# A two-layer attention block: shift rows on SyncE's queue and turned once more per unit, lead maxima in written order, modulation jobs one at a time

## The chip, the cores and the metric

The kernel runs on one core of a Trainium2 chip. The metric is the device time of one execution in microseconds (us). Engines are named as the profile names them: PE (TensorE, matrix products), DVE (VectorE), ACT (ScalarE), POOL (GpSimd) and SP (SyncE, which here only issues DMAs). Each engine runs its own instructions in program order and waits on semaphores for the others.

## The reference, cut to what matters

Two layers over 1024 latent tokens and 256 context tokens, width 1024. Layer 0 is grouped-query attention with 16 heads of 64 and 4 key heads, layer 1 is latent attention with 16 heads. Each has a normalisation that is scaled and shifted by a condition, and a gate path.

```python
def hybrid_layer(x, ctx, c, c_ctx, w_mod, b_mod, norm_w, mixer, mixer_params, cos, sin, with_ctx_out):
    shift, scale, gate = adaln_params(c, w_mod, b_mod)
    shift_c, scale_c, gate_c = adaln_params(c_ctx, w_mod, b_mod)
    h = rms_norm(x, norm_w) * (1.0 + scale[:, None, :]) + shift[:, None, :]
    hc = rms_norm(ctx, norm_w) * (1.0 + scale_c) + shift_c
    y, yc = mixer(h, hc, mixer_params, cos, sin, with_ctx_out)
    x = x + gate[:, None, :] * y
    if with_ctx_out:
        ctx = ctx + gate_c * yc
    return x, ctx

def gqa_attend(q, k, v):
    s = jnp.einsum('bqhgd,bkhd->bhgqk', q, k).astype(jnp.float32) * (GQA_HEAD_DIM ** -0.5)
    p = jax.nn.softmax(s, axis=-1).astype(v.dtype)
    return jnp.einsum('bhgqk,bkhd->bqhgd', p, v)
```

The modulation of layer 1 (`adaln_params`: silu(c) times a matrix) does not depend on layer 0, so the kernel computes it between the work of layer 0.

## The kernel before

**Stages.** A plan (0 to about 262 us) works out norms, projections, query and key rotations and most gates of layer 0: every piece of work is put down with a slot, and the pieces are issued in order of their slots. A tile of queries takes four slots (24 products of PE, then on DVE `hss`, `h_ms`, `t`, `tl` and the scaled `t` of L1123, which PE transposes at L1131), and some tiles carry a piece of a weight split (`wb`, L152). Among them stand the modulation jobs: `cols_fetch` loads a block of layer 1's modulation matrix, `cols_mult` (L1342) multiplies it with the condition of the latent and of the context tokens, by `mod_cols` (L251 to L254): one DVE product over 1024 columns for each, with the sum as a column. Later jobs (`some_cols`) follow until 311 us with the last gate slices.

**Lead.** Then come twelve gate slices (`gate_slice`, 512 or 256 tokens by 128 gate columns, 24 products each, named `mm`), among which the maxima of the first two attention units are to be taken, two after each slice but the last, up to 14 (L1505 to L1519). A maximum (`mx`, L475 for latent keys, L480 for context keys) is a pair of products of queries and keys, and a DVE reduction. PE's order in this stage is the scheduler's.

**Attention of layer 0** (`Attention.run`) goes through 20 units, numbered from 0: 16 heads over all 1280 keys, and four units of context tokens over 256 keys (numbers 4, 9, 18 and 19). For each unit: scores `st` for a block of 128 keys at a time (L589), exponentials `p` on ACT (L596), then the products with v, `avt` (L650). Ahead of the unit that is worked on, the maxima of the units behind it are taken among the scores. The sums of the exponentials are added up on POOL (`acp`, L636), turned on DVE to a row `rrow`, which goes to DRAM and comes back over all rows as `rb`; the gate comes as `sg`; POOL multiplies `rb` with `sg` and the result `os` with `rb` (L733, L734), and `od` (L738) stores it. In PE, DVE, ACT and POOL the order is the written one here; that of SP's DMAs is the scheduler's.

**Shift rows.** Scores are shifted by the maximum before the exponential, by one more product: `st<-shift,minus` (L589), where `shift` holds the negated maxima of four heads as rows. `do_shift` (L499 to L512) reduces a unit's maxima on DVE to `top` and puts a `turn` in a list: four 32 x 32 transposes on DVE (`turn_squares`, L95) and two DMAs (L510) that write the row into `shift`. In layer 0 `shift` is a single tile that all units share: a row's write waits until the products of the unit before have read the tile, and the next unit's first product with it waits for the row. In layer 1 each unit has such rows in a tile `QS` of its own. `run_turns(next_turn)` runs the turns of the list up to unit `next_turn`: the next unit, or the one behind the context units that follow. Before the change it is called once in a unit, between its scores and its products with v. The DMAs go out on ACT's queue while `run` works (`self.running`), else on SP's:

```python
for n in range(2):
    (act if self.running else sp).dma_start(raw(s["crow"][n]), r[4 * n:4 * n + 4, :])
```

**Loads.** Keys of a key head are KA and KB (L1418), queries of a unit QA and QL (L1395, L1396), all on SP's queue. The keys' room in SBUF becomes free when the last modulation job of `some_cols` is done.

Of the kernel before, what the change touches and what calls it, by code (L numbers as in the profile page):

```python
# [12 lines left out]
BF16 = mybir.dt.bfloat16  # L13
# [6 lines left out]
P = 128  # L20
D = 1024
# [8 lines left out]
WIDE = (True, False)  # L30


def raw(ap):
    return ap.bitcast(F32)
# [3 lines left out]
def hybrid_kernel(ctx: ExitStack, tc: tile.TileContext, ins: dict, out: bass.AP):  # L38
    nc = tc.nc
    pe, act, dve, pool, sp = nc.tensor, nc.scalar, nc.vector, nc.gpsimd, nc.sync  # L40
# [50 lines left out]
    def turn_squares(dst, src):  # L91

        w = src.shape[-1]
        for g in range(4):
            dve.transpose(dst[:, w * g:w * g + w], src[32 * g:32 * g + 32, :])  # L95
# [96 lines left out]
    class ModPart:  # L192
# [6 lines left out]
        def __init__(self, l, sec, part, n, pool_of, bufs, rowp, ps_mod, ps_tp):  # L199
            self.l, self.sec, self.part, self.n = l, sec, part, n  # L200
            self.pool_of, self.bufs, self.rowp, self.ps_mod, self.ps_tp = pool_of, bufs, rowp, ps_mod, ps_tp
            self.st = {}
# [45 lines left out]
                dve.tensor_tensor(s1, tv, bias, op=ALU.add)  # L248
                dve.scalar_tensor_tensor(A[l][:, ks, :], s1, 1.0, nw, op0=ALU.add, op1=ALU.mult)

    def mod_cols(w, u, junk, sec, k, conds=2):  # L251

        for j in range(conds):
            dve.scalar_tensor_tensor(junk, w, 0.5, u[:, j, :], op0=ALU.mult, op1=ALU.mult, accum_out=sums_of[sec][:, k, j:j + 1])  # L254

    def mod_cols_end(sec):

        t = sums_of[sec]
        if sec == 2:
            dve.tensor_add(raw(tops[3][:, :KT]), t[:, :, 0], colsT[:, 1, 16:24])  # L260
            r = turned[96:128, :]
            turn_squares(r, raw(tops[3]))
            sp.dma_start(gated[1][0:1, :].rearrange("o (k p) -> (o k) p", p=P), r[:KT, :])
            return
        bias = colsT[:, 1, 8 * sec:8 * sec + 8].unsqueeze(2).broadcast_to([P, KT, 2])
        if sec == 0:
            dve.tensor_tensor(Bv[1], t, bias, op=ALU.add)
        else:
            nw = colsT[:, 1, 24:32].unsqueeze(2).broadcast_to([P, KT, 2])
            dve.tensor_tensor(t, t, bias, op=ALU.add)  # L270
            dve.scalar_tensor_tensor(A[1], t, 1.0, nw, op0=ALU.add, op1=ALU.mult)
# [77 lines left out]
    class Attention:  # L349
        def __init__(self, l, units, ops):  # L350
            self.l, self.units, self.ops = l, units, ops
            self.state = {}
            self.vcache = {}
            self.kcache = {}
            self.sm = sm_pool
            self.step = 0
            self.deferred = []
            self.totals = []
            self.sums = 0
            self.running = False  # L360
            self.turns = []
            self.started = 0
            self.done = 0
            self.todo = []
            self.last_lat = [u for u in units if u["kind"] == "lat"][-1]
# [133 lines left out]
        def do_shift(self, u):  # L499

            s = self.state[id(u)]
            m = tops[self.units.index(u) % 4]
            dve.reduce_max(m[:, :8], s["m"], axis=AX.X)

            def turn():
                at_ = 32 * (self.units.index(u) % 2)
                r = turned[at_:at_ + 32, :]
                turn_squares(r, raw(m))
                for n in range(2):
                    (act if self.running else sp).dma_start(raw(s["crow"][n]), r[4 * n:4 * n + 4, :])  # L510

            self.turns.append((self.units.index(u), turn))  # L512

# [232 lines left out]
        def run(self, lead, ahead, extra, tail):  # L746

            count = lead
            parts = None
            self.running = True  # L750
            with tc.manual_schedule(engines={mybir.EngineType.PE, mybir.EngineType.DVE, mybir.EngineType.Activation, mybir.EngineType.Pool}):
                for t, u in enumerate(self.units):
                    kts = u["kts"]
# [6 lines left out]
                    next_turn = t + 1  # L760
                    while next_turn + 1 < len(self.units) and len(self.units[next_turn]["kts"]) <= 4:
                        next_turn += 1
                    if not WIDE[self.l]:
                        next_turn = None

                    def one_more():
# [156 lines left out]
    right = dict(side="right", reuse_waits="tile")  # L923
# [7 lines left out]
    small = stR.enter_context(tc.tile_pool(name="sml0", bufs=3, **right))  # L931
# [5 lines left out]
    plan = Plan()  # L937
# [379 lines left out]
    gate_in = {}  # L1317
# [21 lines left out]
        sp.dma_start(w, ins["l1_w_mod_t"][sec * D + k * P:sec * D + (k + 1) * P, :])  # L1339
        gate_in[k] = w  # L1340

    def cols_mult(sec, k):  # L1342
        mod_cols(gate_in.pop(k), gate_in["u"], small.tile([P, D], BF16, name="junk", tag="junk", bufs=1), sec, k)

    plan.at(46, more_room)
    at_step = 47.6
# [10 lines left out]
    for j in range(2):  # L1357
        plan.at(72.5 + 4 * j, cond_rows, j)
    for k in range(KT):
        plan.at(77 + 7 * k, cols_fetch, 0, k)  # L1360
        plan.at(82.2 + 7 * k, cols_mult, 0, k)
    plan.at(138, mod_cols_end, 0)
    weight("g1", 2048, 120, (120.2, 122.2, 124.2, 127.2), (125.2, 127.1, 129.2, 132.2))
    for m in range(2):
# [109 lines left out]
    at = Attention(0, units, dict(scale=0.125, load=l0_load, scores=l0_scores, maxima=l0_maxima, mparts=1, open=l0_open, gaps=(4, 8, 11), kbufs=2, qbufs=3, vw=256))  # L1474
# [3 lines left out]
    u = mw.tile([P, 2, D], F32, name="urow", tag="urow", bufs=1)  # L1478
    for j in range(2):
        sp.dma_start(u[:, j, :], ud[j:j + 1, :].broadcast_to([P, D]))  # L1480
    junk = mw.tile([P, D], BF16, name="junk", tag="junk", bufs=1)
    blocks = [(sec, k) for sec in (1, 2) for k in range(KT)]

    def some_cols(n):

        for _ in range(n):
            sec, k = blocks.pop(0)
            w = mw.tile([P, D], F32, name="wcols", tag="wcols")
            sp.dma_start(w, ins["l1_w_mod_t"][sec * D + k * P:sec * D + (k + 1) * P, :])
            mod_cols(w, u, junk, sec, k, 3 - sec)  # L1490
            if k == KT - 1:
                mod_cols_end(sec)

    with tc.tile_pool(name="wkg0a", bufs=4, **right) as wkg:
        for m in range(2, 4):
            for s0 in range(0, NT, 512):
                gate_slice(0, 0, m, s0, min(512, NT - s0), ws["g0"], hT, ps_mm, wkg)
                some_cols(2)
# [7 lines left out]
        pieces.pop(0)()()  # L1506
    stG.close()
    at.open_early(stE)
    at.start_unit()
    with tc.tile_pool(name="wkg0b", bufs=2, **right) as wkg:  # L1510
        for m in range(4):
            for s0 in range(0, NT, 512) if m else (1024,):
                gate_slice(0, 1, m, s0, min(512, NT - s0), ws["g1"], hT, ps_mm, wkg)
                if (m, s0) != (3, 1024):
                    at.maxima(min(at.done + 2, 14), 2)
                at.step += 1
                at.run_turns()
                if s0 == 512:
                    pieces.pop(0)()()  # L1519
# [5 lines left out]
    first = []  # L1525
# [47 lines left out]
    with ExitStack() as st:  # L1573
# [3 lines left out]
        small = st.enter_context(tc.tile_pool(name="sml1a", bufs=3, **right))  # L1577
# [56 lines left out]
    with ExitStack() as st:  # L1634
# [3 lines left out]
        small = st.enter_context(tc.tile_pool(name="sml1b", bufs=3, **right))  # L1638
# [180 lines left out]
    for p_ in range(8):  # L1819
        for par in range(2):  # L1820
# [3 lines left out]
    at = Attention(1, units, dict(scale=float(96 ** -0.5), load=l1_load, scores=l1_scores, maxima=l1_maxima, mparts=2, open=l1_open, gaps=(4, 6, 9),  # L1824
                                  kbufs=3, qbufs=3, vw=128))
    stE = ExitStack()

    with ExitStack() as st:
# [3 lines left out]
        small = st.enter_context(tc.tile_pool(name="sml1c", bufs=3, **right))  # L1832
# [145 lines left out]
    first = []  # L1978
# [57 lines left out]
```

## Time and profile before

| | us |
|---|---|
| median of three runs (lowest, highest) | 1651.92 (1649.15, 1654.16) |
| the profiled execution | 1649.71 |
| its span on the core | 1647.9 |

| engine | busy us | share of the span |
|---|---|---|
| PE | 1603.8 | 97% |
| DVE | 1142.0 | 69% |
| POOL | 957.7 | 58% |
| ACT | 642.2 | 39% |

PE is nearly always at work. In the page's row of the granted clock every slice reads 9, so the losses are small and scattered: they are read from PE's waits by cause and from windows of 20 us. In a row of the timeline the columns are the start, the duration, the engine, the line, the operation, the tiles (out <- in), and in brackets how long the engine was idle before it and what ended that. "SPq" and "ACTq" are instructions that issue a DMA: their duration is the issue, not the transfer.

### The profile page before, as it was taken

Reading aid. Unit: us, or ns where it says so; the run is one execution under the profiler, and the core shown is the slowest. Engines: PE = TensorE matmul, PEld = TensorE weight load, DVE = VectorE, ACT = ScalarE, POOL = GpSimd, SP = SyncE. Lnnn points to the kernel's source line nnn. Section 1 sums busy time; section 2 is a strip of 40 time slices with the busy share of each in tenths; the row PEclk is TensorE's granted clock in tenths of the full one; section 3 lists DMA queues with packets and bytes.
Section 4 is the critical chain, followed back from the end, with each engine's and each line's share of the span. In section 5 each row is a group of like instructions: output and inputs, shape, how many; then the busy total and the mean of one; then the engine's idle time right before and its main releaser. Section 6 shows DMA issues by size and latency. Waiting matters only on the chain.

```text
span 1647.9 us, 26555 instructions
## 1 busy us (share of the span) xinstructions
PE 1603.8 (97%) x9836; PEld 1181.2 (72%) x9836; DVE 1142.0 (69%) x1939; ACT 642.2 (39%) x943; POOL 957.7 (58%) x628
## 2 busy tenths in 40 slices
PE   8999899999999999989999999999999999999998
PEld 5776788775555555557887899887766767767587
DVE  3765986678898888716566667765788788788231
ACT  4643221125554655422234543341534444435310
POOL 2773540118899899933334555450768778777521
PEclk9999999999999999999999999999999999999999
DMA  9545667851444332257324776777566565563451
GB/s 320 178 137 180 186 186 234 247 144 46 107 96 107 97 98 78 59 145 223 119 77 131 214 234 174 221 204 196 127 150 143 136 136 121 136 144 76 124 182 66
DMA packets 215358, 246.26 MB, mean 149 GB/s; under 512 B 19962, under 2 KB 157426, under 8 KB 215228
## 3 DMA queue, kind: packets, MB, share of 16 engines
q1 hardware_dynamic: 214260, 244.31, 53.3%
q8 instruction: 78, 1.28, 0.3%
q14 instruction: 52, 0.43, 0.1%
q10 hardware_dynamic: 968, 0.25, 0.1%
HBM read 170.71 MB, written 73.63 MB: 148 GB/s over the span
## 4 chain that ended last, share of the span: by engine, by line
PE 81%; DVE 6%; DMA 5%; POOL 4%; issue 2%; ACT 1%; SPq 1%; ACTq 0%; DVEq 0%; POOLq 0%
PE st L589 19%; PE av L650 8%; PE mm L109 7%; PE avt L650 7%; PE mm L110 7%; PE mm L111 7%; PE mx L441 4%; PE y L109 3%; PE y L111 3%; PE y L110 3%; PE mx L475 2%; DVE wb L152 1%; POOL acp L636 1%; PE mx L451 1%; DVE t L1123 1%
## 5 line engine op out<-in xcount | busy, mean ns | idle before, releaser
L636 POOL TENSOR_TENSOR acp<-acp,p 128x1024 f32<-128x1024 f32 x188 | 448.8, 2387 | 12.6
L596 ACT ACTIVATE p<-st 128x1024 f32<-128x1024 f32 x328 | 336.4, 1027 | 165.0 <-PE st L589 156.4
L443 DVE TENSOR_REDUCE m<-mx 128x1 f32<-128x512 f32 x256 | 175.6, 691 | 65.3 <-PE mx L441 59.4
L636 POOL TENSOR_TENSOR acp<-p 128x1024 f32<-128x1024 f32 x34 | 81.5, 2398 | 201.3 <-ACT p L596 201.2
L484 DVE TENSOR_REDUCE m<-mx 128x1 f32<-128x1024 f32 x128 | 150.8, 1220 | 45.6 <-PE mx L475 44.7
L650 PE MATMUL avt<-p,v 128*64 128x512 f32 x672 | 149.4, 596 | 0.0
L650 PE MATMUL av<-p,v 128*64 128x512 f32 x640 | 141.1, 595 | 0.0
L152 POOL TENSOR_TENSOR wb<-wraw,wa 128x512 fp32r<-128x512 f32 (+3 forms) x65 | 91.1, 1415 | 77.3 <-ACT wa L173 77.2
L109 PE MATMUL mm<-wa,hh 128*128 128x512 f32 (+2 forms) x336 | 125.5, 373 | 2.0 <-ACT hh L1023 2.0
L589 PE MATMUL st<-QH,KH 64*128 64x512 f32 x320 | 122.7, 407 | 0.1
L111 PE MATMUL mm<-wa,hl 128*128 128x512 f32 (+2 forms) x336 | 120.9, 360 | 1.4 <-DVE hl L1026 1.4
L110 PE MATMUL mm<-wb,hh 128*128 128x512 f32 (+2 forms) x336 | 120.6, 359 | 0.0
L589 PE MATMUL st<-QH,KL 64*128 64x512 f32 x320 | 118.1, 391 | 0.0
L589 PE MATMUL st<-QL,KH 64*128 64x512 f32 x320 | 117.7, 390 | 0.0
L109 PE MATMUL y<-wa,oh 128*128 128x512 f32 (+1 forms) x296 | 114.1, 386 | 2.0 <-DVE yt L880 1.4
L111 PE MATMUL y<-wa,ol 128*128 128x512 f32 (+1 forms) x296 | 113.5, 384 | 0.6 <-DVE ol L863 0.6
L110 PE MATMUL y<-wb,oh 128*128 128x512 f32 (+1 forms) x296 | 113.5, 383 | 0.0
L650 PEld LDWEIGHTS avt<-p,v 128*64 128x64 f32 x672 | 46.3, 137 | 93.2 <-issue 85.0
L650 PEld LDWEIGHTS av<-p,v 128*64 128x64 f32 x640 | 44.4, 137 | 87.9 <-issue 87.3
L109 PE MATMUL mm<-hh,wa 128*128 128x512 f32 (+1 forms) x264 | 104.0, 394 | 0.0
L110 PE MATMUL mm<-hl,wa 128*128 128x512 f32 (+1 forms) x264 | 102.5, 388 | 0.0
L111 PE MATMUL mm<-hh,wb 128*128 128x512 f32 (+1 forms) x264 | 102.1, 387 | 0.0
(259 smaller groups left out, 4026.7 us busy)
## 6 DMA issues: line engine op xcount, KB each, us to landing
wraw<-in_l_w_in SPq DMA_DIRECT2D x28, 512.0 KB
wcols<-in_l_w_mod_t SPq DMA_DIRECT2D x24, 512.0 KB
KH<-k1h SPq DMA_DIRECT2D x32, 320.0 KB
KL<-k1l SPq DMA_DIRECT2D x32, 320.0 KB
rb<-rrow SPq DMA_DIRECT2D x72, 128.0 KB
mraw<-in_l_w_mod SPq DMA_DIRECT2D x16, 512.0 KB
wraw<-in_l_w_out SPq DMA_DIRECT2D x16, 512.0 KB
QA<-q0h SPq DMA_DIRECT2D x32, 256.0 KB
```

Of the source, the lines that this page charges most:

```text
L109: pe.matmul(ps, lhsT=lh(k), rhs=rh(k), start=first and i == 0, stop=False)
L110: pe.matmul(ps, lhsT=lh(k), rhs=rl(k), start=False, stop=False)
L111: pe.matmul(ps, lhsT=ll(k), rhs=rh(k), start=False, stop=last and i == len(ks) - 1)
L152: eng.tensor_sub(lo, a, b)
L441: pe.matmul(held["m"][:, cs], lhsT=q[:, t * P:(t + 1) * P], rhs=k[:, ks], start=j == 0, stop=j == len(pairs) - 1)
L443: dve.reduce_max(s["m"][:, i, n:n + 1], held["m"], axis=AX.X)
L475: pe.matmul(m[:, n * 512:n * 512 + 512], lhsT=q[:, i * P:(i + 1) * P], rhs=k[:, n * 512:n * 512 + 512], start=True, stop=True)
L484: dve.reduce_max(s["m"][:, i, 0:1], m, axis=AX.X)
L589: pe.matmul(ps[:, n * 512:(n + 1) * 512], lhsT=lh, rhs=rh, start=j == 0, stop=j == last)
L596: act.activation(p, ps, AF.Exp, scale=self.ops["scale"])
L636: pool.tensor_add(t, a, b)
L650: pe.matmul(s["av"][64 * n:64 * n + 64, :], lhsT=s["v"][:, kt, u["vc"]:u["vc"] + 64], rhs=p[:, n * 512:(n + 1) * 512], start=kt == kts[0], ...
```

## The change

Four things are changed.

1. The rows of `turn` go out on SP's queue always, in both layers (`self.running` is gone).
2. In `run`, for layer 0 (`WIDE`), `run_turns(next_turn)` is called at the start of each unit too, ahead of its scores. `next_turn` is the next unit, or the one behind the context units that follow.
3. In the lead, both units are started at once, PE's order is the written one, and the slices (0, 1024) and (1, 0) carry no maxima: the first two stand behind slice (1, 512).
4. The modulation jobs of the plan are one product at a time: five blocks are at 82.2 + 8k and four slots later, the other three at 121.5 + 5(k - 5) and two slots later, where there was a pair at 82.2 + 7k.

```diff
-    def mod_cols(w, u, junk, sec, k, conds=2):
-
-        for j in range(conds):
+    def mod_cols(w, u, junk, sec, k, conds):
+
+        for j in conds:
             dve.scalar_tensor_tensor(junk, w, 0.5, u[:, j, :], op0=ALU.mult, op1=ALU.mult, accum_out=sums_of[sec][:, k, j:j + 1])
...
-                    (act if self.running else sp).dma_start(raw(s["crow"][n]), r[4 * n:4 * n + 4, :])
+                    sp.dma_start(raw(s["crow"][n]), r[4 * n:4 * n + 4, :])
...
-                    if not WIDE[self.l]:
+                    if WIDE[self.l]:
+                        self.run_turns(next_turn)
+                    else:
                         next_turn = None
...
-    def cols_mult(sec, k):
-        mod_cols(gate_in.pop(k), gate_in["u"], small.tile([P, D], BF16, name="junk", tag="junk", bufs=1), sec, k)
+    def cols_mult(sec, k, j):
+        mod_cols(gate_in[k], gate_in["u"], small.tile([P, D], BF16, name="junk", tag="junk", bufs=1), sec, k, (j,))
...
-        plan.at(77 + 7 * k, cols_fetch, 0, k)
-        plan.at(82.2 + 7 * k, cols_mult, 0, k)
+        first = 82.2 + 8 * k if k < 5 else 121.5 + 5 * (k - 5)
+        plan.at(first - 5, cols_fetch, 0, k)
+        for j in range(2):
+            plan.at(first + (4 if k < 5 else 2) * j, cols_mult, 0, k, j)
...
-    at.start_unit()
-    with tc.tile_pool(name="wkg0b", bufs=2, **right) as wkg:
+    for _ in range(2):
+        at.start_unit()
+    with tc.tile_pool(name="wkg0b", bufs=2, **right) as wkg, tc.manual_schedule(engines={mybir.EngineType.PE}):
         for m in range(4):
             for s0 in range(0, NT, 512) if m else (1024,):
                 gate_slice(0, 1, m, s0, min(512, NT - s0), ws["g1"], hT, ps_mm, wkg)
-                if (m, s0) != (3, 1024):
+                if (m, s0) > (1, 0) and (m, s0) != (3, 1024):
                     at.maxima(min(at.done + 2, 14), 2)
```

**SP's queue behind unit 6.** Before the change, SP's rows stand so from the store of unit 3 on (`128x2x256` is the store of unit 4, the context unit; QA and QL are the queries of a unit that is loaded ahead):

```order
L738 DMA od_109<-os 64x512 x2
L728 DMA sg<-sgd_107 64x512 [waits DMAHW4_49,DMAHW1_49,Pool_49]
L738 DMA od_109<-os 128x2x256 [waits Pool_49]
L728 DMA sg<-sgd_107 64x512
L1395 DMA QA<-q0h 64x1024 [waits PE_49]
L1396 DMA QL<-q0l 64x512 [waits DMAHW5_49,PE_49]
L1395 DMA QA<-q0h 64x1024 [waits DMAHW7_49]
L702 DMA rrow<-turned 32x32 [waits DMAHW1_49,DVE_49]
```

and after it:

```order
L737 DMA od_109<-os 64x512 [waits DMAHW7_49]
L737 DMA od_109<-os 64x512 [waits DMAHW0_49]
L727 DMA sg<-sgd_107 64x512 [waits DMAHW4_49,DMAHW1_49,Pool_49]
L737 DMA od_109<-os 128x2x256 [waits Pool_49]
L727 DMA sg<-sgd_107 64x512
L1397 DMA QA<-q0h 64x1024 [waits PE_49]
L509 DMA shift<-turned 1x4x128 [waits DMAHW5_49,DVE_49,PE_49]
L509 DMA shift<-turned 1x4x128 [waits DMAHW6_49,PE_49]
L1398 DMA QL<-q0l 64x512 [waits DMAHW7_49]
L701 DMA rrow<-turned 32x32 [waits DMAHW0_49,DVE_49]
```

The two rows of `shift` (L509 there; the change takes a line out above) were not on SP. Now they stand behind the gate loads `sg`, behind the store `od` that waits for POOL, and behind the first half of a QA load.

**PE in the lead.** Before the change, PE's rows at the first maximum (the products of slice (2, 0), with `hh`, on both sides of it):

```order
L109 MATMUL mm<-hh,wa 128x512
L110 MATMUL mm<-hl,wa 128x512
L111 MATMUL mm<-hh,wb 128x512
L475 MATMUL mx<-KA,QA 128x512 [waits DMAHW7_49,DMAHW3_49,PE_49]
L475 MATMUL mx<-KA,QA 128x512
L109 MATMUL mm<-hh,wa 128x512
L110 MATMUL mm<-hl,wa 128x512
L111 MATMUL mm<-hh,wb 128x512
L109 MATMUL mm<-hh,wa 128x512
```

and after it (the products of slice (1, 512) ahead, and those of (1, 1024), with `hhc`, behind):

```order
L109 MATMUL mm<-hh,wa 128x512
L110 MATMUL mm<-hl,wa 128x512
L111 MATMUL mm<-hh,wb 128x512
L474 MATMUL mx<-KA,QA 128x512 [waits DMAHW7_49,DMAHW3_49,PE_49]
L474 MATMUL mx<-KA,QA 128x512 [waits DMAHW5_49,DMAHW0_49]
L474 MATMUL mx<-KA,QA 128x512 x2
L109 MATMUL mm<-hhc,wa 128x256 [waits DVE_49]
L110 MATMUL mm<-hlc,wa 128x256
L111 MATMUL mm<-hhc,wb 128x256
```

The first maximum stood behind half of slice (2, 0), with one maximum at a place; now two stand together behind slice (1, 512), with slice (1, 1024) and all of (2, 0) behind them.

**DVE among the query tiles.** Before the change, where the first job stands (`junk` is the product of a job):

```order
L103 TENSOR_TENSOR tl<-tp,th 128x512 [waits DMAHW3_49,Activation_49]
L254 SCALAR_TENSOR_TENSOR junk,cols_69<-wcols,urow 128x1024 [waits DMAHW5_49]
L254 SCALAR_TENSOR_TENSOR junk,cols_69<-wcols,urow 128x1024 [waits DVE_49]
L1123 TENSOR_TENSOR t_1829<-t_1829,h_rs 128x512 [waits Pool_49]
L1104 TENSOR_REDUCE hss<-sq 128x8 [waits Activation_49]
L133 TENSOR_SCALAR h_ms<-hss 128x8 [waits DVE_49]
L1110 TENSOR_TENSOR t_1883<-mm,rope_q 128x512 [waits DMAHW2_49]
L1116 TENSOR_TENSOR t_1885<-mm,rope_q 128x16x16 x2
```

and after it:

```order
L103 TENSOR_TENSOR tl<-tp,th 128x512 [waits DMAHW3_49,Activation_49]
L254 SCALAR_TENSOR_TENSOR junk,cols_69<-wcols,urow 128x1024 [waits DMAHW5_49]
L1123 TENSOR_TENSOR t_1829<-t_1829,h_rs 128x512 [waits DVE_49,Pool_49]
L1104 TENSOR_REDUCE hss<-sq 128x8 [waits Activation_49]
L133 TENSOR_SCALAR h_ms<-hss 128x8 [waits DVE_49]
L1110 TENSOR_TENSOR t_1880<-mm,rope_q 128x512 [waits DMAHW2_49]
L1116 TENSOR_TENSOR t_1882<-mm,rope_q 128x16x16 x2
L103 TENSOR_TENSOR tl<-tp,th 128x512 [waits DMAHW7_49,Activation_49]
L254 SCALAR_TENSOR_TENSOR junk,cols_69<-wcols,urow 128x1024
L1123 TENSOR_TENSOR t_1880<-t_1880,h_rs 128x512 [waits Pool_49]
```

The second product of the job moved behind the `tl` of the next tile.

More of the change, by code (lines that the diff above doesn't have):

```diff
@@ L359, in __init__ @@
             self.sums = 0
-            self.running = False
             self.turns = []
@@ L749, in run @@
             parts = None
-            self.running = True
             with tc.manual_schedule(engines={mybir.EngineType.PE, mybir.EngineType.DVE, mybir.EngineType.Activation, mybir.EngineType.Pool}):
@@ L1489, in some_cols @@
             sp.dma_start(w, ins["l1_w_mod_t"][sec * D + k * P:sec * D + (k + 1) * P, :])
-            mod_cols(w, u, junk, sec, k, 3 - sec)
+            mod_cols(w, u, junk, sec, k, range(3 - sec))
             if k == KT - 1:
```

## The prediction

> **What bounds the kernel now.** I read the page first, then PE's waits by cause, then the windows in which those waits lie, then the timelines around each.
>
> ```profile
> span 1647.9 us, 26555 instructions
> ...
> PE 1603.8 (97%) x9836; PEld 1181.2 (72%) x9836; DVE 1142.0 (69%) x1939; ACT 642.2 (39%) x943; POOL 957.7 (58%) x628
> ```
>
> TensorE is busy 97% of the span. The change removes no matmul, so it can gain only what PE loses to waiting and to its clock, and it can lose any amount by a new wait. PE's waits by cause (total us, times, longest):
>
> ```profile
> PE tp L1131 <- DVE t L1123: 7.6, 7, 2.3
> PE st L589 <- DMA shift<-turned: 7.6, 3, 5.1
> ...
> PE mx L475 <- issue: 2.8, 1, 2.8
> ...
> PE mx L475 <- DMA QA<-q0h: 1.1, 1, 1.1
> ```
>
> These four are the ones that the change touches: the query phase of layer 0 (L1131), the shift rows (L589), the lead maxima and the queries' loads (L475). The windows below give PE, PEld, DVE, ACT and POOL busy, then the granted clock.
>
> ```profile
> 160.00:180.00 20.00, 19.05 (x91) 15.21 (x90) 16.87 (x28) 5.55 (x10) 9.65 (x7) 1.00 0.77 233
> 180.00:200.00 20.00, 18.10 (x83) 14.13 (x81) 19.86 (x30) 6.67 (x12) 13.84 (x9) 1.00 0.49 150
> 200.00:220.00 20.00, 17.75 (x78) 14.75 (x79) 18.40 (x29) 4.00 (x7) 11.94 (x8) 0.91 0.51 145
> 220.00:240.00 20.00, 19.65 (x94) 15.95 (x93) 16.12 (x29) 4.16 (x7) 6.18 (x4) 1.00 0.61 182
> ...
> 320.00:340.00 20.00, 18.10 (x64) 10.60 (x64) 11.39 (x11) 1.58 (x3) 0.00 (x0) 0.83 0.64 157
> ...
> 520.00:540.00 20.00, 17.55 (x96) 8.45 (x96) 14.22 (x24) 6.32 (x8) 17.11 (x9) 0.91 0.32 82
> ...
> 700.00:720.00 20.00, 14.86 (x104) 8.33 (x102) 3.00 (x4) 6.51 (x7) 8.78 (x6) 0.83 0.50 136
> ```
>
> A wait costs more than itself: 0.91 over 20 us is 0.09 x 20 = 1.8 us of lost clock behind waits of 2 us, and 0.83 is 3.4 us, of which the wait covers a part. I charge 1.7 us for a stall of 2 us or more. The Trainium skill (TensorE: Matmul & The Clock Gate, "What's actually happening") asks for a wholly idle window of about 3.4 us before the clock halves. The trace disagrees, since a wait of 2.16 us was enough (the row at 536.56 below); by the page, two of my clock charges (0.9 us each, below) would fall away and the sum would be 1.7 us less.
>
> **Part 1, the query phase: -4.9 us.** A modulation job is two products in a row on DVE:
>
> ```profile
> 193.61 1.21 DVE L254 SCALAR_TENSOR_TENSOR junk<-wcols,urow 128x1024 bf16<-128x1024 f32 x1
> ...
> 194.87 1.22 DVE L254 SCALAR_TENSOR_TENSOR junk<-wcols,urow 128x1024 bf16<-128x1024 f32 x1
> ```
>
> The pair holds DVE 2.4 us. In the four windows from 160 to 240, DVE is busy 71.2 of 80 us, but 19.86 of 20 where PE waits. Six pairs, twelve products, stand among the query tiles now; after the change it is ten single ones, a tile apart, so that a tile has at most one product of 1.2 us more and no window should be full. In the two crowded windows PE is idle for 4.15 us, most of the 7.6; with the 1.8 of clock 6.0 us can go. The job that lands on a tile with a weight split still makes that tile late, so I take 4.9, between 2 and 6. The later jobs go into the gate tiles, where PE waits for nothing now.
>
> **Part 2, the lead: +4.2 us.**
>
> ```profile
> 313.06 0.39 PE L111 MATMUL mm<-hh,wb 128*128 128x512 f32 x1
> ...
> 321.90 1.19 PE L475 MATMUL mx<-KA,QA 64*128 64x512 f32 x2 [2.83 <-issue]
> ```
>
> ```profile
> 312.17 1.16 SPq L1418 DMA_DIRECT2D KA<-k0h  x2
> ```
>
> The keys' load is issued at 312.17, behind the release of the modulation room, and the first maximum can start at 321.90. Now two gate slices (313.3 to 319.06) run before it; in the written order the first pair stands right behind slice (1, 512), which ends at 313.3, and PE takes its instructions in order. The second half of the queries comes 1.7 us later (an estimate from the spacing of the loads), and the pair needs both halves. So PE stops from 313.3 to 323.4, 10.1 us, plus 1.7 of clock. Gone are the 2.8 us wait and its 3.4 us of clock. Seven visits of two maxima replace fourteen of one:
>
> ```profile
> 331.61 0.50 PE L109 MATMUL mm<-hh,wa 128*128 128x512 f32 x1
> 331.95 0.40 PE L110 MATMUL mm<-hl,wa 128*128 128x512 f32 x1
> ```
>
> The first product behind a visit is 0.1 us longer than the next, and I count as much on its other side: 0.2 x 7 = 1.4. Together 10.1 + 1.7 - 2.8 - 3.4 - 1.4 = +4.2. The bounds are 0 (the loads land 4 us sooner) and +6 (no gain from fewer visits).
>
> **Part 3, the rows on SP.** A row is two DMAs, and every row of layer 0 goes into one tile. The first product with that tile in a unit's scores waits for every write before it. On ACT the rows waited for nothing but DVE's transposes; on SP each stands behind sg, od, sg and half a QA load, and od waits for POOL.
>
> ```profile
> L510 SPq DMA_DIRECT2D shift<-turned x2: 604/650/695, 344.5 to 345.3; - x2
> ```
>
> ```profile
> 685.27 0.31 SPq L702 DMA_DIRECT2D rrow<-turned  x1
> 686.59 1.10 SPq L730 DMA_DIRECT2D rb<-rrow  x2
> ```
>
> An issue on SP costs 0.65 us, a row 1.3. A small write is seen 1.3 us behind its issue on an idle queue (685.27 to 686.59; the rows below have 510.55 to 514.40, 3.85 us, behind loads). I take 1.3 and keep 3.85 as the upper end.
>
> Behind units 6 and 11 a context unit's total is still in POOL's queue:
>
> ```profile
> 492.53 1.29 POOL L734 TENSOR_TENSOR os<-os,rb 128x512 f32<-128x512 f32 x1
> ```
>
> ```profile
> 493.85 0.38 SPq L738 DMA_DIRECT2D od<-os  x1
> ...
> 494.79 0.59 SPq L1395 DMA_DIRECT2D QA<-q0h  x1
> ...
> 588.08 0.60 SPq L1395 DMA_DIRECT2D QA<-q0h  x1
> ```
>
> ```profile
> 490.24 0.46 PE L589 MATMUL st<-shift,minus 64*128 64x512 f32 x2
> ...
> 585.44 0.40 PE L589 MATMUL st<-shift,minus 64*128 64x512 f32 x2
> ```
>
> Unit 6: od goes at 493.85 when POOL is through, QA at 494.79, the row at 495.4, seen at 495.4 + 1.3 + 1.3 = 498.0. PE needs it at 490.24: 7.8 us late, less the 1.5 us by which PE is late already (next paragraph; POOL isn't), so +6.3, +1.7 clock, -1.1 for the wait on QA that falls into it: +6.9. Unit 11: row at 588.7, seen 591.3, needed 585.44: +5.9 and 1.7, +7.6. With the slow landing each is 2.5 us worse; with POOL a microsecond less behind, 1 us better.
>
> The change also turns the next rows at a unit's start, which matters where a context unit is next (units 3, 8 and 17).
>
> ```profile
> 417.96 2.31 DVE L99 TRANSPOSE_TENSOR_REDUCE squares<-p 128x64 f32<-128x2048 f32 x1
> ...
> 687.51 1.68 DVE L95 STREAM_TRANSPOSE turned<-top 32x32 f32<-32x32 f32 x8
> ```
>
> ```profile
> 422.38 0.39 PE L589 MATMUL st<-shift,minus 64*128 64x512 f32 x2
> ...
> 512.68 0.40 PE L589 MATMUL st<-shift,minus 64*128 64x512 f32 x2
> ...
> 536.56 0.76 PE L589 MATMUL st<-shift,minus 64*128 64x512 f32 x1 [2.16 <-DMA shift<-turned]
> ...
> 689.23 0.40 PE L589 MATMUL st<-shift,minus 64*128 64x512 f32 x2
> ...
> 706.89 0.79 PE L589 MATMUL st<-shift,minus 64*128 64x512 f32 x1 [5.14 <-DMA shift<-turned]
> ```
>
> ```profile
> 510.55 0.53 SPq L702 DMA_DIRECT2D rrow<-turned  x1
> ...
> 514.40 1.08 SPq L730 DMA_DIRECT2D rb<-rrow  x2
> ```
>
> - Unit 3: DVE turns unit 4's row behind squares, which ends at 420.3; four transposes (0.21 each) to 421.1, two issues and the landing to 423.7, needed 422.38: **+1.5** (0 to 2.5).
> - Unit 8, start: unit 9's row stands behind rb, which waits for rrow. By the old time of rb (514.40) it lands at 514.95 + 1.3 + 1.3 = 517.5, 4.9 late; with fewer loads ahead of rrow it is 1.3 behind it and the row 1.8 late. I take +3.0 and 0.9 of clock, **+3.9**. Unit 8, end: the wait of 2.16 goes with its rows gone ahead, 0.3 before it and 1.7 of clock: **-4.2**.
> - Unit 17: the wait of 5.14 and its clock go, -6.8. Rows 18 and 19 now go ahead of unit 17's scores: DVE is done at 689.2, the fourth issue at 691.0 (the first starts at 688.4), seen 692.3, needed 689.23: +3.0, with 0.9 of clock. **-2.9** (-5 to -0.5).
>
> Part 3 sums to 1.5 + 6.9 + 7.6 + 3.9 - 4.2 - 2.9 = **+12.8**, between +6 and +19.
>
> **ACT freed, and layer 1: 0.** Layer 1's rows move to SP too:
>
> ```profile
> 1195.24 1.22 ACTq L510 DMA_DIRECT2D QS<-turned  x2
> ```
>
> ```profile
> 1204.34 0.40 PE L589 MATMUL st<-QS,KS 33*128 33x512 f32 x2
> ```
>
> From the rows' issue to their use lie 9.1 us, and each unit has a QS tile of its own, so it waits for no older product. Less 1.3 for its issues and 3.85 for a slow landing, 3.9 us are left, room for six issues of 0.65 ahead of it. If that cover were gone, each further issue would cost 0.65 us in each of 15 units. ACT loses DMAs alone, and PE doesn't wait for ACT here. The Trainium skill (DMA: Bandwidth & Descriptors, "Issuing engines are not separate DMA queues") says that the issuing engine only decides the sequencer's time. No row here contradicts that for the transfer itself, but the od row at 493.85 shows what stands ahead of it in SP's program.
>
> **Sum.** -4.9 + 4.2 + 12.8 = +12.1 us on the profiled execution's 1649.7 (span 1647.9): 1661.8. The median of the runs shown is 2.2 us above that execution, within the spread of the three, and I leave that out: **1662**.
>
> **Rivals.**
>
> *The rows are in time (faster).* If SP reaches them while PE runs a unit's products with v, and POOL isn't behind at units 6 and 11, the new waits fall away: -4.9 + 4.2 - 4.2 - 6.8 - 1.1 = -12.8, 1637. For it: at most boundaries SP's list ends early. Against it: od at 493.85 and the need at 490.24. It decides where POOL's os ends 6 us sooner. By the page on DMA queues this would be the result, since the queue makes no difference by it. Chance 0.12.
>
> *One boundary holds (no change).* POOL is caught up at one of units 6 and 11, because PE came late before it: 1661.8 - 7.6 = 1654. Chance 0.23.
>
> *Every boundary is marginal (worse).* The landing is the slow one, 2.5 us more behind QA, and units 6, 8, 11 and 17 take it: +10, 1672, less where a stall lets POOL and SP catch up. Chance 0.15.
>
> *It isn't what it says.* "Once more per unit" changes only what a context unit's row does (units 3, 8, 17); at other units the second call finds nothing new. This is in the sum.
>
> My forecast has the remaining 0.50. About 0.3% (5 us) is what a measurement tells from no change: faster is under 1647, slower is over 1657. The chances: faster 0.12, same 0.23, slower 0.65. The range runs from 1648 (all lower ends but one) to 1671 (the worse rival), with the faster rival outside.
>
> **What would show it.** In the changed profile, right: a wait of PE for shift of 5 to 8 us once behind unit 6 and once behind unit 11, with od on SP just ahead; a wait of about 10 us at the first lead maximum near 308 us; no wait of 5 us near 700; few waits on L1123 t. Wrong: shift waits that are few and short; a first maximum that finds its keys; DVE waits in the query phase of the old size; a wait on QS in layer 1.

## The result and the profile after

The changed kernel takes 1668.45 us (median of 4 runs, 1665.71 to 1670.39), the kernel before 1651.76 (1649.15 to 1654.16): a ratio of 1.010, 95% interval 1.0077 to 1.0123, or 16.7 us slower. The forecast was 1662 and slower; the time lies in its range, near the upper end, and closer to the 1672 of the worse rival than to 1662. The profiled execution took 1670.39 us, 20.7 more than the one of before.

The page of the changed kernel, the span and PE's busy time:

```profile
span 1668.6 us, 26566 instructions
...
PE 1608.1 (96%) x9836; PEld 1197.3 (72%) x9836; DVE 1145.3 (69%) x1939; ACT 640.4 (38%) x943; POOL 955.4 (57%) x628
```

PE's waits by cause (total us, times, longest):

```profile
PE st L588 <- DMA shift<-turned: 14.9, 5, 6.5
PE mx L474 <- DMA QA<-q0h: 9.5, 2, 8.4
PE tp L1131 <- DVE t L1123: 7.2, 8, 1.3
...
PE y L109 <- DVE yt L880: 3.7, 1, 3.7
```

The number of products is the same; the waits have grown. Those on shift rows have doubled, the first lead maximum waits 8.4 us, and the waits on DVE's scaled t, which the fourth part was to shorten, are as many and as long in sum as before (7.6 in 7). The windows of the query phase and of the lead, columns as in the prediction:

```profile
180.00:200.00 20.00, 18.09 (x86) 14.42 (x85) 19.56 (x29) 6.67 (x12) 13.07 (x9) 1.00 0.61 184
200.00:220.00 20.00, 17.89 (x85) 14.33 (x84) 19.81 (x31) 4.59 (x8) 11.06 (x8) 1.00 0.43 129
...
300.00:320.00 20.00, 12.97 (x66) 10.73 (x64) 11.79 (x25) 1.58 (x3) 0.00 (x0) 0.93 0.88 262
320.00:340.00 20.00, 17.52 (x79) 13.57 (x80) 7.99 (x8) 0.98 (x2) 0.00 (x0) 0.82 0.76 192
```

DVE is as full as before from 180 to 220 us, but with no halved clock (1.00 for 0.91). In the lead PE has lost 7 us in one window and 2.5 in the next.

Where the time went is read by setting the same instruction of both timelines side by side: the last transposes of the query phase, the first product with v of each unit, the last product. Differences of the two profiled executions, in us:

| stretch | forecast | measured |
|---|---|---|
| up to the first query tile (59 us) | 0 | +1.5 |
| query phase | -4.9 | -2.0 |
| lead, up to unit 0's products with v | +4.2 | +2.9 |
| unit 3, start | +1.5 | +1.4 |
| behind unit 6 | +6.9 | +6.8 |
| unit 8, start | +3.9 | +3.7 |
| unit 8, end | -4.2 | -4.3 |
| behind unit 11 | +7.6 | +9.2 |
| unit 17, start and end | +3.9 - 6.8 | +2.8 - 6.8 |
| unit 19 to layer 1's first unit | 0 | +4.3 |
| layer 1 | 0 | +1.4 |

The smaller differences between units make up the rest. Three of the rows, +1.5, +4.3 and +1.4, are put down to the profiled executions further below. Without their 7.2 us the profiled difference is 13.5 us, for 12.1 forecast.

Behind unit 6, SP's queue, then POOL's and PE's timelines of the changed kernel:

```profile
486.84 1.23 SPq L737 DMA_DIRECT2D od<-os  x2
494.15 0.46 SPq L727 DMA_DIRECT2D sg<-sgd  x1
495.49 0.38 SPq L737 DMA_DIRECT2D od<-os  x1
...
496.43 0.60 SPq L1397 DMA_DIRECT2D QA<-q0h  x1
497.14 1.38 SPq L509 DMA_DIRECT2D shift<-turned  x2
```

```profile
492.83 1.29 POOL L732 TENSOR_TENSOR rb<-rb,sg 128x512 f32<-128x512 f32 x1
494.20 1.26 POOL L733 TENSOR_TENSOR os<-os,rb 128x512 f32<-128x512 f32 x1
```

```profile
499.90 0.98 PE L588 MATMUL st<-shift,minus 64*128 64x512 f32 x2 [5.90 <-DMA shift<-turned]
...
601.81 0.97 PE L588 MATMUL st<-shift,minus 64*128 64x512 f32 x2 [6.53 <-DMA shift<-turned]
```

SP stands still from 488.1 to 494.15. Then sg goes as POOL's product with `rb` ends (494.12), od as that with `os` ends (495.46), then QA and the row, and PE starts 1.4 us behind the end of the row's second issue. It had waited 5.9 us, and behind unit 11 in the same way 6.5.

### The profile page after: what moved, and what is told of

It reads as the page before. It is cut to its first block, busy times and chain, and to the rows that moved or that the text cites. A ratio compares the mean times of both kernels' runs of the same rounds, so it can differ in the third digit from the quotient of the medians.

```text
span 1668.6 us, 26566 instructions
## 1 busy us (share of the span) xinstructions
PE 1608.1 (96%) x9836; PEld 1197.3 (72%) x9836; DVE 1145.3 (69%) x1939; ACT 640.4 (38%) x943; POOL 955.4 (57%) x628
## 4 chain that ended last, share of the span: by engine, by line
PE 78%; DVE 8%; POOL 4%; DMA 4%; issue 3%; SPq 1%; ACT 1%; ACTq 0%; DVEq 0%; POOLq 0%
PE st L588 18%; PE av L649 8%; PE mm L109 7%; PE mm L111 7%; PE mm L110 7%; PE avt L649 5%; PE mx L440 4%; PE y L109 4%; PE y L111 4%; PE y L110 4%; PE mx L474 2%; DVE junk L254 2%; POOL acp L635 1%; DVE wb L152 1%; DVE m L485 1%
## 5 line engine op out<-in xcount | busy, mean ns | idle before, releaser
L635 POOL TENSOR_TENSOR acp<-acp,p 128x1024 f32<-128x1024 f32 x188 | 448.0, 2383 | 12.5
```

The lines of the kernel that those rows point to most:

```text
L635: pool.tensor_add(t, a, b)
```

## The experiments

Each comes with the runs of the kernel before on the same chip, whose median was between 1646.9 and 1649.8 us; ratios are to those.

### The four parts alone

**Rows on SP.**

```diff
-                    (act if self.running else sp).dma_start(raw(s["crow"][n]), r[4 * n:4 * n + 4, :])
+                    sp.dma_start(raw(s["crow"][n]), r[4 * n:4 * n + 4, :])
```

> Only the first part of the change: the shift rows of both layers go out on SP's queue. Theory A (SP stands waiting for POOL at sg and od, behind units 6 and 11, with the rows behind them): the two waits of about 6 us on shift are there without the other parts, and the time is 14 to 17 us over the kernel before (1666 to 1669 us). Rival B (the rows are late only because DVE is asked for a second turn, SP itself holds nothing up): no wait for shift over 2.5 us except the old one behind unit 17, and 1650 to 1654 us.

1659.1 us, ratio 1.0078 (1.0061 to 1.0094): 11.8 us between the medians. PE's waits in its profile:

```profile
PE st L588 <- DMA shift<-turned: 16.8, 4, 6.3
```

The two waits are there, of 6.15 and 6.27 us, so rival B is out. By the medians it is less than theory A's 14 to 17 (the interval of the ratio reaches to 15.5), and an old wait is gone too: the one behind unit 8, though no turn was made early. SP issues the four rows in 2.67 us, and ACT had needed 7.53.

```profile
535.00 2.67 SPq L509 DMA_DIRECT2D shift<-turned  x4
```

```profile
525.10 7.53 ACTq L510 DMA_DIRECT2D shift<-turned  x4
```

(The first row is of this run, the second of the kernel before.) Each DMA signals its end on one of a few semaphores (lanes, `DMAHW` in the rows of the order), which ACT's and SP's DMAs use in turn, and the next one on a lane waits for that signal. In the trace of the kernel before, ACT's second, third and fourth issue start at 529.10, 530.29 and 532.05, each within 0.1 us of the end of an SP transfer on the lane that it waits for (529.08, 530.21 and 532.03), so it is SP's `sg` and `od` that stretched ACT's issues. This unit's end is shorter by 4.3 us here, as it is with the early turn. But in the four kernels that leave the rows and turns alone (the third and the fourth part by themselves, and two versions below) it is shorter too, by 1.7 to 2.5 us: part of the old wait is of the one profiled execution, and the rest can be had by SP's queue or by the early turn. In layer 1 this kernel keeps its distance to the kernel before from the first unit's products with v (+7.9) to the last (+7.9): its rows on SP cost nothing there.

**Turns at each unit's start, on ACT's queue.**

```diff
-                    if not WIDE[self.l]:
+                    if WIDE[self.l]:
+                        self.run_turns(next_turn)
+                    else:
                         next_turn = None
```

> Only the second part: the turns run at the start of each unit of layer 0 too, the rows stay on ACT's queue. Theory A: the old waits of 2.2 us (unit 8) and 5.1 us (unit 17) go with their halved clock, about 11 us, but 4 us of it is lost again at the first output products, whose rows come from a chain that didn't move, and units 3, 8 and 17 start 1 to 4 us late: 1646 to 1653 us. Rival B (the early turn costs nothing where ACT issues it and all of the waits is gained): 1640 to 1642 us.

1647.05 us, ratio 1.0001 (0.9986 to 1.0016): no change.

```profile
PE st L589 <- DMA shift<-turned: 5.6, 5, 2.3
```

The old wait of 5.1 us is gone, and five smaller ones stand there. By the units' starts, unit 3 loses 4.2 us, unit 8 gains 4.3 at its end and loses 2.0 at its start, unit 17 gains 6.8 and loses 4.2. Theory A's range held. What is left, 2.3 us over layer 0's attention, is too small to be seen in the medians.

**The lead.**

```diff
-    at.start_unit()
+    for _ in range(2):
+        at.start_unit()
...
+    with tc.tile_pool(name="wkg0b", bufs=2, **right) as wkg, tc.manual_schedule(engines={mybir.EngineType.PE}):
...
-                if (m, s0) != (3, 1024):
+                if (m, s0) > (1, 0) and (m, s0) != (3, 1024):
```

> Only the third part: the lead with PE in written order and its first two maxima behind slice (1, 512). Theory A: PE waits 8 to 9 us for the first queries, the old 2.8 us wait and its slow clock go, some switches less: 2 to 4 us over the kernel before (1654 to 1656 us). Rival B (the profiled 2.9 us is between executions, the lead is free): within 1 us of the kernel before.

1653.0 us, ratio 1.0033 (1.002 to 1.0046): 5.7 us between the medians, above theory A's 2 to 4; rival B is out.

```profile
PE mx L475 <- DMA QA<-q0h: 11.3, 3, 9.2
```

The first pair waits 9.2 us for the first half of the queries and 1.0 for the second, 10.2 in all, as the prediction had it (10.1).

**The jobs.**

```diff
-        plan.at(77 + 7 * k, cols_fetch, 0, k)
-        plan.at(82.2 + 7 * k, cols_mult, 0, k)
+        first = 82.2 + 8 * k if k < 5 else 121.5 + 5 * (k - 5)
+        plan.at(first - 5, cols_fetch, 0, k)
+        for j in range(2):
+            plan.at(first + (4 if k < 5 else 2) * j, cols_mult, 0, k, j)
```

> Only the fourth part: the modulation jobs of the plan one product at a time. Theory A (DVE is the bound from 160 to 220 us whatever the order, spreading only saves the halved clock): 2 us less than before (1649 to 1651 us), four or so waits on L1123 of about 1 us each in place of two of about 2. Rival B (the prediction's: crowding is what makes PE wait): 5 us less (1646 to 1647 us), few waits.

1645.67 us, ratio 0.9995 (0.9982 to 1.0008): 1.6 us less by the medians, near theory A, but not clear of no change. (The profiled execution took 1651.61, the longest of its ten, so single instructions are read from it and not the time.) The products' summary (duration ns: least, median, most), first of the kernel before and then of this run:

```profile
L254 DVE SCALAR_TENSOR_TENSOR junk<-wcols,urow x16: 1212/1224/2279, 169.7 to 249.5; 128x1024 bf16<-128x1024 f32 x16
```

```profile
L254 DVE SCALAR_TENSOR_TENSOR junk<-wcols,urow x16: 1214/2293/2347, 172.6 to 253.2; 128x1024 bf16<-128x1024 f32 x16
```

In pairs most products took 1.22 us (14 of 16); one at a time most take 2.29. Their place in this run's timelines, DVE's and then POOL's, tells why:

```profile
193.72 2.31 DVE L254 SCALAR_TENSOR_TENSOR junk<-wcols,urow 128x1024 bf16<-128x1024 f32 x1
195.96 0.08 DVE L254 DVE_READ_ACCUMULATOR junk<-wcols,urow 128x1 f32 x1
195.96 0.68 DVE L1123 TENSOR_TENSOR t<-t,h_rs 128x512 f32<-128x512 f32 x1
```

```profile
193.20 1.74 POOL L152 TENSOR_TENSOR wb<-wraw,wa 128x512 fp32r<-128x512 f32 x1
```

The product runs beside POOL's weight split (193.20 to 194.94), and the scaled t behind it is free of POOL and takes 0.68. In the kernel before, the pair of this tile (193.61, shown in the prediction) stood behind the scaled t, which met POOL's split (191.40 to 193.15) itself:

```profile
191.91 1.78 DVE L1123 TENSOR_TENSOR t<-t,h_rs 128x512 f32<-128x512 f32 x1
```

Taken together, 11.8 + 5.7 - 1.6 and -0.2 for the turns are 15.7 us by the medians (17.6 by the four ratios), for the 16.7 of the whole change: the parts add.

### Jobs behind the scaled t

```diff
-        first = 82.2 + 8 * k if k < 5 else 121.5 + 5 * (k - 5)
+        first = 83.2 + 8 * k if k < 5 else 121.5 + 5 * (k - 5)
```

> The kernel before with the fourth part alone, its first five blocks one slot later (83.2 + 8k), so that a product stands behind DVE's scaled t and not ahead of it. Theory E (single products lie beside POOL's work on the same tile and take 2.31 us for 1.21, which takes back what the spreading gives): they take 1.2 us again, the waits on L1123 of about 1 us mostly go, and it is 3 to 5 us under the kernel before. Rival F (DVE's whole load sets the pace from 160 to 220 us, wherever the products stand): as with the fourth part as it is, within 2 us of the kernel before, with the waits of about 1 us.

1647.54 us, ratio 0.9985 (0.997 to 1.0). The products' summary, and DVE's timeline at the same tile:

```profile
L254 DVE SCALAR_TENSOR_TENSOR junk<-wcols,urow x16: 1210/1218/2309, 172.1 to 250.6; 128x1024 bf16<-128x1024 f32 x16
```

```profile
191.98 1.77 DVE L1123 TENSOR_TENSOR t<-t,h_rs 128x512 f32<-128x512 f32 x1
193.67 1.21 DVE L254 SCALAR_TENSOR_TENSOR junk<-wcols,urow 128x1024 bf16<-128x1024 f32 x1
```

The products take 1.21 us again, but now the scaled t stands beside POOL's split and takes 1.77. From 180 to 220 us three waits of about 1 us remain of four, and the query phase gains 3.0 us on the kernel before where the fourth part as it is gained 2.0. Theory E was right on the products and wrong on the waits. The median is 2.3 us under the kernel before, short of E's 3 to 5, but with an interval from 5 to 0 the time doesn't decide between E and F. What the rows show is that in each tile with a split some DVE instruction pays for the overlap.

### What holds the rows

**Rows of units 7 and 12 on ACT** (in the changed kernel):

```diff
-                    sp.dma_start(raw(s["crow"][n]), r[4 * n:4 * n + 4, :])
+                    (act if WIDE[self.l] and self.units.index(u) in (7, 12) else sp).dma_start(raw(s["crow"][n]), r[4 * n:4 * n + 4, :])
```

> The changed kernel, with the rows of units 7 and 12 alone (those that stand on SP behind the totals of the context units) sent on ACT's queue again. Theory A (SP's place behind sg and od is what makes them late): both waits of 6 us on shift go, with their clock, 15 to 17 us less than the changed kernel, so 4 to 6 us or less over the kernel before. Rival B (the rows are late because DVE turns them late, whatever the queue): the waits stay, within 2 us of the changed kernel.

1654.47 us, ratio 1.0026 (1.0016 to 1.0036).

```profile
PE st L588 <- DMA shift<-turned: 5.5, 2, 4.4
```

Both waits of 6 us are gone, and with them 12 of the 16.7 us: 4.6 are left, as theory A has it, though it put what goes at 15 to 17. DVE turns these rows where it did. So their place on SP is what made them late. One wait has grown: at the start of unit 8 the early row of unit 9 is waited for for 4.4 us, and not 1.3.

**Two buffers for sg** (in the changed kernel), to tell sg from od:

```diff
-                sg = op.tile([P, 512], F32, name="sg", tag="sg", bufs=1)
+                sg = op.tile([P, 512], F32, name="sg", tag="sg", bufs=2 - l)
```

> The changed kernel with two buffers for sg in layer 0 only; od still waits for POOL ahead of the rows. Theory A says that od ends last: sg is issued about 6 us sooner, od at the same time behind POOL, and the waits on shift behind units 6 and 11 stay at 5.5 to 6.5 us each. Rival D (sg is the hold, od waits only because sg was late): the waits fall below 2 us.

One run, 1664.23 us. The waits behind units 6 and 11 are 5.88 and 6.05:

```profile
PE st L588 <- DMA shift<-turned: 14.7, 5, 6.0
```

```profile
487.41 6.24 SPq L727 DMA_DIRECT2D sg<-sgd  x2
494.52 0.37 SPq L737 DMA_DIRECT2D od<-os  x1
```

od goes when POOL's `os` is done and ends last, as theory A said. But the edit freed less than was meant: the second issue of the first row is already a later load of sg, hoisted to this place, and it waits for POOL too (it goes at 493.18, when POOL's product with `rb` ends). So od is last by its place, and a queue without a hold by sg wasn't tried.

**SP not held** (in the changed kernel): the same, and the context units' od issued by POOL.

```diff
-                    sp.dma_start(dst, view(o[rows, :]))
+                    (sp if lat else pool).dma_start(dst, view(o[rows, :]))
```

> The changed kernel, rows on SP as it has them, but SP is no longer held: sg has two buffers in layer 0, so that its load needn't wait for POOL's product, and a context unit's od is issued by POOL. The queries' load still stands ahead of the rows. Theory A: both waits of 6 us go, 14 to 17 us less than the changed kernel, 0 to 5 us over the kernel before. Rival C (the queries' load ahead of the rows in the queue makes their landing slow): the waits stay at 3 us or more, at least 6 us over the kernel before.

1660.26 us, ratio 1.0061 (1.0044 to 1.0079); the waits are 4.93 and 5.00. By the expectations that is rival C. The queue shows that it isn't:

```profile
488.24 6.98 SPq L727 DMA_DIRECT2D sg<-sgd  x3
495.31 0.54 SPq L1397 DMA_DIRECT2D QA<-q0h  x1
495.96 1.38 SPq L509 DMA_DIRECT2D shift<-turned  x2
```

```profile
498.91 0.97 PE L588 MATMUL st<-shift,minus 64*128 64x512 f32 x2 [4.93 <-DMA shift<-turned]
```

SP is still held, by the second of three loads of sg, which goes at 494.11: with the room that the edit made, the scheduler put the gate load of one more unit ahead of QA, and its buffer comes free with POOL's product of the context unit, which ends at 494.08. The row goes 1.2 us sooner, and PE starts 1.6 us behind the end of its issue. So the experiment failed to lift the hold, and QA stands ahead of the row in both kernels. What QA ahead costs is in the changed kernel's trace: by its semaphores the second DMA of the row at 497.14 lands 2.15 us behind the start of its issue, and that of the row at 522.76, with no QA just ahead, 1.67 behind. That is half a microsecond of a wait of 6, so rival C falls by the landing, not by the time.

### The change without its first part

All rows on ACT's queue, the other three parts as in the change.

```diff
-                    sp.dma_start(raw(s["crow"][n]), r[4 * n:4 * n + 4, :])
+                    (act if self.running else sp).dma_start(raw(s["crow"][n]), r[4 * n:4 * n + 4, :])
```

> The changed kernel without its first part: all rows on ACT's queue as before, with the early turns, the lead and the jobs of the change. If the parts simply add (rows 11.8, turns 0, lead 5.7, jobs -0.8 us, each run alone), 4 to 6 us over the kernel before, with no wait for shift behind units 6 and 11. Rival G (the parts lean on each other: the early turns need SP's queue, and on ACT's they hold the exponentials): 8 us or more over it, by waits at the starts of units 3, 8 and 17.

1650.26 us, ratio 1.0021 (1.0009 to 1.0033), 3.3 us over the kernel before, below the 4 to 6 that were expected, and no wait for shift is over 2.3 us. Rival G is out, and the rows on SP are 13.4 of the 16.7 us when they are taken out of the whole change.

### Versions that mend

**The first pair behind slice (2, 0)** (the third part alone):

```diff
-                gate_slice(0, 1, m, s0, min(512, NT - s0), ws["g1"], hT, ps_mm, wkg)
-                if (m, s0) > (1, 0) and (m, s0) != (3, 1024):
-                    at.maxima(min(at.done + 2, 14), 2)
+                two = lambda: at.maxima(min(at.done + 2, 14), 2)
+                gate_slice(0, 1, m, s0, min(512, NT - s0), ws["g1"], hT, ps_mm, wkg,
+                           between={KT // 2: two} if (m, s0) in ((2, 512), (3, 0)) else {})
+                if (m, s0) > (1, 1024) and (m, s0) != (3, 1024):
+                    two()
```

> The third part alone, PE in written order, but its first two maxima stand behind slice (2, 0), where the keys and queries are about to land, and two pairs stand in the middle of slices. Theory A (only the place of the first pair costs: PE waits there from 313 to 322 us): a wait of 2 us or less at the first pair, and 0 to 4 us under the kernel before. Rival H (pairs of maxima in written order cost by themselves, by waits for DVE's reductions and the two buffers): 2 us or more over the kernel before.

1642.31 us, ratio 0.9961 (0.9948 to 0.9975): faster by 4.6 us by the medians, a little more than theory A's 0 to 4, and rival H is out.

```profile
PE mx L475 <- DMA QA<-q0h: 2.4, 2, 1.2
```

In the lead the wait is 1.2 us (the other 1.2 stands at 496 us and is old). Written order and pairs don't cost; the place of the first pair did. (Two pairs stand in the middle of slices here, which wasn't tried by itself.)

**Rows and jobs mended**: the kernel before with the rows on SP but for units 7 and 12, without early turns, and the jobs at 83.2 + 8k (the two edits as above).

> The kernel before with two things taken from the change and mended: rows on SP's queue, but those of units 7 and 12 on ACT's, no early turns; and the jobs one at a time behind the scaled t. Theory A: no wait for shift behind units 6 and 11, 4 us less behind unit 8 (whose four rows waited on ACT for free lanes), 1 to 3 us less from the jobs: 4 to 8 us under the kernel before. Rival I (SP's other rows take as much as ACT's lanes did): within 2 us of it.

1641.72 us, ratio 0.9967 (0.9955 to 0.9978).

```profile
PE st L588 <- DMA shift<-turned: 4.7, 4, 3.9
```

No wait behind units 6, 8 and 11 is over 0.4 us; one of 3.9 stays at unit 17's end.

**All of it together**: the last two kernels in one.

> Both mended versions together: the lead with its first pair behind slice (2, 0), the rows on SP but for units 7 and 12, the jobs one at a time behind the scaled t. Theory A (the parts lie in different stages and add): 9 to 11 us under the kernel before, a ratio of 0.993 to 0.995, with one wait at the first maximum of 2 us or less. Rival J (one stage gives back what another gains): less than 7 us under it.

1634.95 us, ratio 0.9921 (0.9908 to 0.9934), 13.1 us under the kernel before and by the two ratios 1.8% under the changed one, where 9 to 11 us were expected. Its page:

```profile
span 1633.5 us, 26562 instructions
...
PE 1595.8 (98%) x9836; PEld 1178.9 (72%) x9836; DVE 1141.9 (70%) x1939; ACT 641.6 (39%) x943; POOL 956.0 (59%) x628
```

The lead's wait is down to 0.6 us, and no window of it has a halved clock.

## Why the prediction was right, and where it was off

The direction, its cause and its place were right. **Part 3**, the rows on SP, carried the forecast (+12.8) and holds step by step: the profiled attention of layer 0 is 12.5 us longer. The waits behind units 6 and 11 were put at 6.3 and 5.9 us and are 5.9 and 6.5; a row is seen 1.4 us behind the end of its last issue (taken: 1.3). So the worse rival, nearer to the measured time, is not what happened: its landing of 3.85 never came up. Moving two rows back to ACT takes the two waits away, which shows the cause. That od ends last, just behind sg, is read from the timelines. That the hold could be lifted on SP itself wasn't shown, since both edits drew another load into the same place. The close sum is luck in part: behind unit 11 the loss is 1.6 more than forecast, since it exceeds its wait of 6.5 by 2.7 us where 1.7 was charged for the clock, and the start of unit 17 is 1.1 less.

One step of it named the wrong cause. The prediction gave the 4.2 us at the end of unit 8 to the early turn. The rows alone, without it, gain them too, as SP issued the four rows in a third of ACT's time, and kernels with neither gain 1.7 to 2.5 there. The early turn by itself is worth nothing, as it gives back at the starts of units 3, 8 and 17 what it gains at the ends.

**Part 1**, the query phase, is the term that was mis-sized: -4.9 was forecast, -2.0 profiled, and the part alone gives 1.6 us by the medians, with no change inside its interval. The failed step is "a tile has at most one product of 1.2 us more": ahead of the scaled t, where the change puts it, a product takes 2.3 us beside POOL. The rows that the prediction quoted (1.21 and 1.22) are of a pair behind the scaled t. The kernel before already had two products of the longer kind, 2.19 us at 183.11 and 2.28 at 217.69, both beside POOL. What came true of the term is the halved clock alone.

**Part 2**, the lead, was put at +4.2; the part alone gives 5.7 by the medians and 4.3 in its profile, the change's own profile 2.9. The wait is as worked out. The clock behind it differs from one execution to the next: from 320 to 340 us it is 0.72 with the part alone and 0.82 in the changed kernel. And the same stretch differs by -1.5 to +1.3 us from the kernel before in kernels whose lead is the old one, so one profile does not fix this term.

**ACT and layer 1** at nothing: right by the first experiment. The 4.3 us between unit 19 and layer 1, and the 1.4 in layer 1, are put down to the profiled execution and not to the change. Over the profiles of the experiments the first of these stretches differs from the kernel before by -2.5 to +3.3 us, and the kernel that only moves the jobs has +2.2. Layer 1 differs by 0 to 1.6: by 1.4 to 1.6 in the kernels nearest to the change, but by 1.4 too in one that only moves the jobs, and by 0 with the rows alone. The 1.5 up to the first query tile is of this kind as well: every other profile has 0.5 to 2.9 there. Why one execution loses 4 us ahead of layer 1 and another doesn't, stays open.

By the medians the sum of 1661.8 is 6.7 us short of 1668.45. Of these 2.1 are the base: the forecast starts from the profiled 1649.7, and the median is 1651.76. Of the other 4.6 (16.7 measured for 12.1), the parts alone give 3.3 in the query phase and 1.5 in the lead, and part 3 with the turns takes 1.2 back (11.6 for 12.8). The last microsecond is within what two sets of medians differ.

The working has small slips, too small to matter: the end of PE's stop in the lead is 321.90 + 1.7 = 323.6 and not 323.4, unit 3's numbers give +1.3 and not +1.5, and two charges of 0.9 are 1.8 and not 1.7.

## What to carry to other kernels

A small transfer that moves to another queue takes on everything that this queue waits for: read the program order of the queue at each place, and for each entry ahead the engine that it waits on and when that one is done. A written order is worth what its worst place costs, so the first use of a load belongs behind the time at which the load lands, and the same pairs two slices later turned 5.7 us of loss into 4.6 of gain. A price from a profile holds for its place: the same product cost 1.2 us beside an idle POOL and 2.3 beside a busy one.

## What was not expected of the hardware

The clock halved behind a wait of 1.26 us (the start of unit 8) and not behind one of 1.97 (the start of unit 17):

```profile
524.47 0.49 PE L588 MATMUL st<-shift,minus 64*128 64x512 f32 x1 [1.26 <-DMA shift<-turned]
...
710.28 1.06 PE L588 MATMUL st<-shift,minus 64*128 64x512 f32 x2 [1.97 <-issue]
```

```profile
520.00:540.00 20.00, 18.54 (x125) 11.98 (x123) 16.41 (x22) 10.85 (x11) 15.81 (x9) 0.91 0.16 41
...
700.00:720.00 20.00, 17.39 (x98) 7.74 (x96) 11.44 (x27) 6.41 (x7) 16.01 (x8) 1.00 0.16 42
```

So the prediction's charge of 1.7 us for each stall of 2 us or more doesn't hold stall by stall. The Trainium skill (TensorE: Matmul & The Clock Gate, "What's actually happening") describes a free-running window; that the length of a wait doesn't decide alone agrees with it, that 1.26 us can be enough does not agree with its wholly idle window.

DVE and POOL slow each other in some operations. A DVE product of 1024 columns takes 2.31 for 1.21 us and a scaled t of 512 columns 1.77 for 0.68 beside POOL's split: the product's overlap of 1.22 us (193.72 to 194.94) cost it 1.10. In the kernel before POOL pays once. Its product of L1118, 1.29 us in the median, takes 2.38 beside a job's product that keeps its 1.22:

```profile
181.85 1.22 DVE L254 SCALAR_TENSOR_TENSOR junk<-wcols,urow 128x1024 bf16<-128x1024 f32 x1
...
181.84 2.38 POOL L1118 TENSOR_TENSOR t<-t,t 128x512 f32<-128x512 f32 x1
```

So about 1.1 us is paid where two such instructions meet, by one of them or the other. Not every overlap costs: beside POOL's `h_rs` (L135, 1.64 us) a product at 169.74 took 1.22.
